# A two-block transformer kernel: the RWKV inverse from 16-wide blocks, and scan work that moves from GpSimd to VectorE

## Chip, cores and metric
One core of one Trainium2 chip runs the whole program in one launch. The metric is the device time of that execution in microseconds; lower is better.

## What is computed
Two blocks of two layers each on a sequence of 256 tokens with 1024 features, in fp32. Block one has a hybrid mixer, cross attention, a dense feed-forward layer and a mixture of eight experts; block two has an attention layer, an MLP, an RWKV-7 layer and a second MLP. The change touches the RWKV layer alone. Its core is a scan that runs forwards (d = 0) and backwards (d = 1) over the tokens, for 16 heads of 64 features:

```
def rwkv7_scan(r, w, k, v, kk, a):
    def step(state, inp):
        r_t, w_t, k_t, v_t, kk_t, a_t = inp
        sa = einsum('bhvk,bhk->bhv', state, -kk_t)
        state = (state * w_t[:, :, None, :] + sa[..., None] * (kk_t * a_t)[:, :, None, :]
                 + v_t[..., None] * k_t[:, :, None, :])
        return state, einsum('bhvk,bhk->bhv', state, r_t)
...
for d in range(2):
    ...
    o = rwkv7_scan(*ins)
    bonus = sum(rh * kd * r_k, axis=-1, keepdims=True) * vh
    dir_out.append((group_norm(o, gn_w, gn_b) + bonus.reshape(nB, S, D)) * g)
y = dir_out[0] + dir_out[1]
return y @ w_o
```

## The kernel before
The scan is done in chunks of 64 tokens: four chunks, two directions. Inside a chunk the recurrence is a triangular system with a 64x64 matrix per head. The stages of `rwkv` follow one another:

- `rwkv_inputs` (L1364): the projections for receptance, keys, values, decay and gates, by matmuls on TensorE with weights that are split into a high and a low part (L335, L336, L372). It ends with the values vx (L1446, L1447) and the gate's inner projection gT (L448, L1449). `rwkv_low` (L1452) makes the decay and the in-context rate of one direction.
- `rwkv_blocks` (L1475), once per direction: eight groups of two heads. For each, ScalarE takes exponentials, VectorE and GpSimd multiply (L1521 to L1529), TensorE makes the chunk matrices (L1540), VectorE masks them (L1548, L1549), and five DMAs on SP's queue write them to a DRAM scratch `rwscr` (L1553 to L1557). The strictly triangular matrices stay in SBUF as nt (L1545, L1546).
- `rwkv_inverse` (L1565), once per direction: it inverts the unit triangular 64x64 matrices of all heads and chunks. Each one is cut into two 32-wide diagonal blocks. VectorE transposes all blocks so that one partition holds one row position (L1579), solves by substitution in 31 steps of a multiply and an add (L1585, L1587), and transposes back in two forms, xn and xd (L1590, L1591). TensorE then forms the off-diagonal 32x32 block in two small products per matrix (L1600, L1608), which run through one partition group at a time, with ScalarE copies between (L1602, L1610). The result xt is a block-diagonal 128x128 matrix for two heads, which is why it is first set to zero (L1578, GpSimd).
- `rwkv_offset` (L1619), once per chunk: everything of the output that doesn't depend on the scan. The gate's outer projection (L1634, TensorE), and the bonus, the norm's shift and the gate's products, almost all on GpSimd (L1625 to L1644). It also takes the mean off the values (L1627 to L1629).
- `rwkv_chunk` (L1648), for each of four steps once per direction: load of the chunk's matrices (mc, L1657), decay of the state (L1666 on VectorE, L1668 on GpSimd), product with the state (pw), product with the inverse (pu, L1685), new state (L1705) and output (po).
- `rwkv_norm` (L1713), once per step and direction: square on ScalarE, mean, a reciprocal root of twelve small VectorE operations (`rsqrt`, L275 to L294), a product on VectorE (L1721) and two operations on GpSimd, in the last step on VectorE (L1723, L1724).

Then the output is transposed (L1357), multiplied with w_o, and the last MLP follows.

The order of instructions on each engine is fixed at build time: a planner takes operations by priority, where priority is place in the program unless `high_priority(n)` moves a part n places ahead, and plays the engines against a timing model. Both calls of the inverse stand ahead by 800 places. Memory sets limits: lxd and lz (L1588, L1592) have one buffer each, in the pool `ip`, for both directions; the second direction's working tile lies in the pool `kp`, over memory that the blocks have used, and in a buffer that the chunk loads use later (L1315). PSUM has two "mm" banks, two "tr" banks and four "acc" banks.

Of the kernel before, what the change touches and what calls it, by code (L numbers as in the profile page):

```python
# [19 lines left out]
P = 128  # L20
D = 1024
KD = 8
# [86 lines left out]
def constants():  # L109
# [104 lines left out]
class K:  # L214
# [1052 lines left out]
    def rwkv(self, h, hstack, hp):  # L1267
# [5 lines left out]
        with ExitStack() as ctx:  # L1273
# [5 lines left out]
            with ExitStack() as left:  # L1279
                with ExitStack() as right:  # L1280
# [11 lines left out]
                    with self.dense("c", 2, 4, "right", 3):  # L1292
                        lp, vx, gT = self.rwkv_inputs(h, rT, z0, z1, tT, aT, opened,
                                                      lambda lp: self.rwkv_low(bq, lp, 0, tT, aT))
# [3 lines left out]
                    xt = [cp.tile([P, KD * 4, P], F32, name="xt0")]  # L1298
# [9 lines left out]
                    with tc.high_priority(800):  # L1308
                        self.rwkv_inverse(ip, ip.tile([P, 3, 32, 32], F32, name="lanes", tag="lanes"), 0, nt[0], xt[0])
                y = lp.tile([P, KD, 4, 64], F32, name="ry")  # L1310
                with ExitStack() as right:
                    kp = pool(right, "rwk", "right")
                    xt.append(kp.tile([P, KD * 4, P], F32, name="xt1"))
# [15 lines left out]
                    for i, c in enumerate((0, 3, 1, 2)):  # L1329
# [4 lines left out]
                        gw[c] = self.rwkv_offset(kp, t[:, i % 2], c, vx, gT, bon, gn, g2, y)  # L1334
# [3 lines left out]
                    for i in range(4):  # L1338
# [4 lines left out]
                        for d, (po, c) in enumerate(outs):  # L1343
                            self.rwkv_norm(kp, po, c, gw[c][d], y, i == 3)
# [19 lines left out]
    def rwkv_inputs(self, h, rT, z0, z1, tT, aT, opened, low):  # L1364
# [5 lines left out]
        with self.tc.tile_pool(name="rin", bufs=1, side="right", reuse_waits="tile") as mp:  # L1370
# [79 lines left out]
        return lp, vx, gT  # L1450
# [114 lines left out]
    def rwkv_inverse(self, lp, lanes, d, nt, xt):  # L1565
# [12 lines left out]
        nc.gpsimd.memset(xt, 0.0)  # L1578
        nc.vector.transpose(n.rearrange("p t s -> p (t s)"), nt[:, :, 32 * a:32 * a + 32].rearrange("p q t -> p t q"))  # L1579
        for s in (range(31) if d == 0 else range(31, 0, -1)):  # L1580
            ts = slice(s + 1, 32) if d == 0 else slice(0, s)
            js = slice(0, s + 1) if d == 0 else slice(s, 32)
            nt_, nj = ts.stop - ts.start, js.stop - js.start
            tv = tmp[:, :nt_ * nj].rearrange("p (t j) -> p t j", t=nt_)
            nc.vector.tensor_mul(tv, n[:, ts, s:s + 1].to_broadcast([P, nt_, nj]),  # L1585
                                 x[:, s:s + 1, js].to_broadcast([P, nt_, nj]))
            nc.vector.tensor_add(x[:, ts, js], x[:, ts, js], tv)  # L1587
# [3 lines left out]
        nc.vector.transpose(xd.rearrange("p q t -> p t q"), x.rearrange("p t j -> p (t j)"))  # L1591
        zs = lp.tile([P, 32, 32], F32, name="lz")  # L1592
        cb = slice(32 * b, 32 * b + 32)
        zb = [self.bank(t) for t in ("mm", "mm", "tr", "tr")]
        for q0 in (0, 16):
            z = zb[q0 // 16]
            for par in range(2):
                pa, pb = pr(par, a), pr(par, b)
                for q in range(16):
                    nc.tensor.matmul(z[pb, q * 32:(q + 1) * 32], nt[pa, q0 + q, cb],  # L1600
                                     xn[pa, q0 + q], start=True, stop=True, skip_group_check=True)
                last = nc.scalar.copy(zs[pb, q0:q0 + 16], z[pb].rearrange("p (q j) -> p q j", q=16))  # L1602
        for q0 in (0, 16):
            z = zb[2 + q0 // 16]
            for par in range(2):
                pa, pb = pr(par, a), pr(par, b)
                for q in range(16):
                    nc.tensor.matmul(z[pa, q * 32:(q + 1) * 32], zs[pb, q0 + q], xd[pb, q0 + q],  # L1608
                                     start=True, stop=True, skip_group_check=True)
                nc.scalar.copy(xt[pa, q0:q0 + 16, 64 * par + 32 * b:64 * par + 32 * b + 32], z[pa].rearrange("p (q j) -> p q j", q=16))  # L1610
        with self.tc.issue_after(last.ins):
            for i in range(4):
                ps = slice(32 * i, 32 * i + 32)
                if d == 0 or i % 2 == 0:
                    nc.scalar.copy(xt[ps, :, ps], xd[ps])
                else:
                    nc.vector.tensor_copy(xt[ps, :, ps], xd[ps])

    def rwkv_offset(self, kp, gate, c, vx, gT, bon, gn, g2, y):  # L1619
# [6 lines left out]
        m = self.sm.tile([P, KD], F32, name="vm")  # L1626
        nc.vector.reduce_sum(m, vx[:, :, c], axis=AX.X)  # L1627
        nc.vector.tensor_scalar(m, m, 1.0 / 64, None, op0=OP.mult)
        nc.gpsimd.tensor_sub(vx[:, :, c], vx[:, :, c], m[:, :, None].to_broadcast([P, KD, 64]))  # L1629
        out = []  # L1630
        for d in range(2):
            b = self.bank("acc", 4)
# [3 lines left out]
            g = gate[:, d]  # L1636
            nc.scalar.copy(g, b.rearrange("p (f v) -> p f v", f=KD))
            nc.gpsimd.tensor_add(vb[d], vb[d], gn[1])
            if d == 0:
                nc.gpsimd.tensor_mul(y[:, :, c], vb[d], g)  # L1640
            else:
                nc.gpsimd.tensor_mul(vb[d], vb[d], g)
                nc.gpsimd.tensor_add(y[:, :, c], y[:, :, c], vb[d])
            nc.gpsimd.tensor_mul(g, g, gn[0])  # L1644
            out.append(g)
        return out

    def rwkv_chunk(self, kp, mp, d, i, prev, scr, xt, pc, vx, hot):  # L1648
# [14 lines left out]
        if prev is not None:  # L1663
# [4 lines left out]
            nc.gpsimd.tensor_mul(st, prev, pcb)  # L1668
# [15 lines left out]
        for f in range(KD):  # L1684
            nc.tensor.matmul(pu[:, f], xt[:, f * 4 + c], w[:, f], start=True, stop=True, skip_group_check=True)  # L1685
# [27 lines left out]
    def rwkv_norm(self, kp, po, c, gw, y, last):  # L1713

        nc = self.nc
        o, sq = (kp.tile([P, KD, 64], F32, name=n, bufs=b) for n, b in (("ro", 2), ("rq", 1)))
        nc.scalar.activation(sq, po, AF.Square)
        va = self.sm.tile([P, KD], F32, name="gva")
        nc.vector.reduce_sum(va, sq, axis=AX.X)
        r = self.rsqrt(va, KD, 1.0 / 64, 64e-5)  # L1720
        nc.vector.tensor_mul(o, po, r[:, :, None].to_broadcast([P, KD, 64]))  # L1721
        eng = nc.vector if last else nc.gpsimd
        eng.tensor_mul(o, o, gw)  # L1723
        eng.tensor_add(y[:, :, c], y[:, :, c], o)  # L1724
# [83 lines left out]
```

## Time and profile before

| | us |
|---|---|
| three runs: lowest, median, highest | 2703.27, 2704.24, 2707.18 |
| the profiled execution's own time | 2704.2 |
| its span in the trace | 2702.4 |

The times are of the device; the trace is of one further execution. An engine's row says how long it was busy; its name stands ahead (PE is TensorE's matmuls, PEld its weight loads, DVE VectorE, ACT ScalarE, POOL GpSimd, SP the engine that issues the DMAs). A granted clock of 1.00 is 2.4 GHz, 0.50 is 1.2 GHz. Time in brackets is idle time ahead of an instruction and what ended it.

### The profile page before, as it was taken

How to read it: one execution, taken by the hardware profiler on the slowest of the kernel's cores; microseconds unless marked ns; L12 is line 12 of the kernel's file. 1: busy time of each engine (PE TensorE's matmuls, PEld its weight loads, DVE VectorE, ACT ScalarE, POOL GpSimd, SP SyncE). 2: the span in 40 equal slices, each digit the busy share in tenths (PEclk: the TensorE clock that was granted, in tenths of full speed). 3: DMA queues.
4: the chain of work that ended last, by engine and by line, in shares of the span. 5: the costliest groups of instructions: out<-in, count | busy, mean ns of one | idle time of the engine just before them, and what ended most of it. 6: DMA issues, size and time to landing. Idle time of an engine off the chain costs nothing. (4 is left out here: it accounts for less than half of the span.)

```text
span 2702.4 us, 38657 instructions
## 1 busy us (share of the span) xinstructions
PE 2470.9 (91%) x14672; PEld 2127.8 (79%) x14672; DVE 2061.6 (76%) x3025; ACT 1557.5 (58%) x2136; POOL 431.1 (16%) x361
## 2 busy tenths in 40 slices
PE   8889999889999999999999999798997788577998
PEld 7778998868788888888888878587996766376897
DVE  8955556955699899988889898666557959967655
ACT  5445445335577778777777777455444646343443
POOL 3800110830000000000000000000111346542111
PEclk9989999989999999999999999899997888668999
DMA  6433454433699999999999999443553227424452
GB/s 239 166 119 131 172 187 161 132 134 133 218 359 368 332 357 368 344 351 351 354 336 360 355 358 353 147 161 107 174 187 106 98 83 191 118 108 190 161 188 104
DMA packets 229952, 598.69 MB, mean 222 GB/s; under 512 B 14778, under 2 KB 33914, under 8 KB 228476
## 3 DMA queue, kind: packets, MB, share of 16 engines
q1 hardware_dynamic: 229756, 596.12, 63.0%
q8 instruction: 117, 1.92, 0.3%
q14 instruction: 79, 0.65, 0.1%
HBM read 579.27 MB, written 16.81 MB: 221 GB/s over the span
## 5 line engine op out<-in xcount | busy, mean ns | idle before, releaser
L336 DVE TENSOR_TENSOR wl<-wst,wh 128x1024 fp32r<-128x1024 f32 (+2 forms) x1037 | 1254.5, 1230 | 351.7 <-ACT wh L335 333.4
L335 ACT ACTIVATE wh<-wst 128x1024 fp32r<-128x1024 f32 (+2 forms) x1037 | 1077.6, 1055 | 562.3 <-PE ps_mm L372 300.3
L372 PE MATMUL ps_mm<-xT_h,wh 128*128 128x256 f32 x1496 | 434.4, 290 | 28.1 <-DVE xT_l L455 15.4
L372 PE MATMUL ps_mm<-xT_h,wl 128*128 128x256 f32 x1496 | 431.6, 289 | 4.7 <-DVE wl L336 3.8
L372 PE MATMUL ps_mm<-xT_l,wh 128*128 128x256 f32 x1496 | 431.8, 289 | 0.2 <-DVE xT_l L455 0.2
L372 PE MATMUL ps_mm<-wh,gh 128*128 128x512 f32 x880 | 352.1, 400 | 0.0
L372 PE MATMUL ps_mm<-wl,gh 128*128 128x512 f32 x880 | 343.8, 391 | 0.0
L372 PE MATMUL ps_mm<-wh,gl 128*128 128x512 f32 x880 | 343.3, 390 | 0.0
L372 PEld LDWEIGHTS ps_mm<-xT_h,wh 128*128 128x128 f32 x1496 | 295.2, 197 | 35.3 <-DVE xT_l L455 16.3
L372 PEld LDWEIGHTS ps_mm<-xT_h,wl 128*128 128x128 f32 x1496 | 294.8, 197 | 8.5 <-DVE wl L336 5.7
L372 PEld LDWEIGHTS ps_mm<-xT_l,wh 128*128 128x128 f32 x1496 | 294.4, 197 | 1.1 <-DVE xT_l L455 0.4
L372 PEld LDWEIGHTS ps_mm<-wl,gh 128*128 128x128 f32 x880 | 165.1, 188 | 35.7
L372 PEld LDWEIGHTS ps_mm<-wh,gl 128*128 128x128 f32 x880 | 165.5, 188 | 32.7
L372 PEld LDWEIGHTS ps_mm<-wh,gh 128*128 128x128 f32 x880 | 165.3, 188 | 32.9 <-ACT gh L363 0.4
L1150 POOL MEMSET qz<- 64x2048 f32 x1 | 1.8, 1799 | 1159.9 <-DVE gg L1158 1159.9
L372 PE MATMUL ps_acc<-wh,mal 128*128 128x512 f32 x448 | 179.1, 400 | 2.8 <-DVE mal L364 2.8
L372 PE MATMUL ps_acc<-wh,mah 128*128 128x512 f32 x448 | 179.0, 400 | 0.7 <-ACT mah L363 0.7
L372 PE MATMUL ps_acc<-wl,mah 128*128 128x512 f32 x448 | 177.7, 397 | 0.0
L372 PE MATMUL ps_acc<-wh,al 128*128 128x512 f32 x344 | 134.8, 392 | 0.0
L372 PE MATMUL ps_acc<-wl,ah 128*128 128x512 f32 x344 | 134.5, 391 | 0.0
L1259 POOL TENSOR_TENSOR mq<-mr 128x512 f32<-128x512 f32 x32 | 56.2, 1758 | 489.5 <-DVE mr L1257 489.5
L372 PE MATMUL ps_acc<-wh,ah 128*128 128x512 f32 x344 | 116.4, 396 | 2.5 <-ACT ah L363 2.5
(469 smaller groups left out, 4061.9 us busy)
## 6 DMA issues: line engine op xcount, KB each, us to landing
wst<-in_moe_gate SPq DMA_DIRECT2D x112, 1024.0 KB, 6.0
wst<-in_moe_down SPq DMA_DIRECT2D x112, 1024.0 KB, 5.6
wst<-in_moe_up SPq DMA_DIRECT2D x112, 1024.0 KB, 5.6
wst<-in_mlp SPq DMA_DIRECT2D x64, 1024.0 KB, 4.9
wst<-in_mix_in SPq DMA_DIRECT2D x16, 1024.0 KB, 5.0
mc<-rwscr SPq DMA_DIRECT2D x8, 1792.0 KB, 7.3
wst<-in_ffn_gate SPq DMA_DIRECT2D x11, 1024.0 KB, 4.9
wst<-in_ffn_up SPq DMA_DIRECT2D x11, 1024.0 KB, 5.1
```

The lines of the kernel that those rows point to most:

```text
L335: nc.scalar.activation(wh[:, :n], src, AF.Copy)
L336: nc.vector.tensor_sub(wl[:, :n], src, wh[:, :n])
L372: self.nc.tensor.matmul(out, a, b, start=start and i == 0, stop=stop and i == n - 1, skip_group_check=True)
L1150: nc.gpsimd.memset(qz[64:128, :, 0], 0.0)
L1259: nc.gpsimd.tensor_mul(q, r, r)
```

## The change
The 32-wide diagonal blocks are no longer solved whole. VectorE solves two 16-wide blocks inside each in 15 steps, both in one instruction. TensorE then merges twice: the two 16-wide blocks into a 32-wide one, in the two forms that are needed (z1, z3 and z2, new), and the two 32-wide ones into the 64-wide inverse (as before). All these loops now run over the matrices and inside that over two or four partition groups, so that consecutive matmuls are of different groups. They take their PSUM from the two "mm" banks. xt holds only the 64x64 matrices, without the zeros, so that the product with it in `rwkv_chunk` becomes two 64-wide ones. The first direction's inverse has no raised priority any more, the second's is raised by 1600 places.

The gates' products go to ScalarE (bonus) and VectorE, reading the projection from PSUM; the means of the values are taken once, at the end of `rwkv_inputs`; the decay product goes to VectorE; the norm takes both directions of a step together, with one reciprocal root for both, and stays on VectorE.

```diff
+        c.add(f"half{d}", (i % 32 // 16 != d).astype(np.float32))
...
-                    with tc.high_priority(800):
-                        self.rwkv_inverse(ip, ip.tile([P, 3, 32, 32], F32, name="lanes", tag="lanes"), 0, nt[0], xt[0])
+                    self.rwkv_inverse(ip, ip.tile([P, 3, 32, 32], F32, name="lanes", tag="lanes"), 0, nt[0], xt[0])
...
-                    with tc.high_priority(800):
+                    with tc.high_priority(1600):
...
+            vm = lp.tile([P, KD, 4], F32, name="vm")
+            nc.vector.reduce_sum(vm, vx, axis=AX.X)
+            nc.vector.tensor_scalar(vm, vm, 1.0 / 64, None, op0=OP.mult)
+            nc.vector.tensor_sub(vx, vx, vm[:, :, :, None].to_broadcast([P, KD, 4, 64]))
...
-        nc.gpsimd.memset(xt, 0.0)
+        for par in range(2):
+            nc.gpsimd.memset(xt[pr(par, b), :, 32 * a:32 * a + 32], 0.0)
...
-        for s in (range(31) if d == 0 else range(31, 0, -1)):
...
+        for s in (range(15) if d == 0 else range(15, 0, -1)):
...
+            tv = tmp[:, :2 * nt_ * nj].rearrange("p (u t j) -> p u t j", u=2, t=nt_)
+            xv = two(x, t0, [32, nt_], j0, [1, nj])
+            nc.vector.tensor_mul(tv, two(n, t0, [32, nt_], s, [0, nj]), two(x, s, [0, nt_], j0, [1, nj]))
+            nc.vector.tensor_add(xv, xv, tv)
...
+        for q in range(32):
+            for ps in grp:
+                nc.tensor.matmul(z1[ps, q], nt[ps, q, 32 * a:32 * a + 32], xn[ps, q, low], start=True, stop=True,
+                                 skip_group_check=True)
+        nc.scalar.activation(zh[:, :, low], z1, AF.Copy, scale=self.c(f"half{d}"))
+        z3 = self.bank().rearrange("p (q j) -> p q j", q=32)
+        for q in range(32):
+            for par in range(2):
+                ps = pr(par, a)
+                nc.tensor.matmul(z3[ps, q], xd[ps, q], zh[ps, q, low], start=True, stop=True, skip_group_check=True)
...
+            nc.vector.tensor_add(xn[ps, :, low], xn[ps, :, low], z3[ps])
+        z2 = self.bank().rearrange("p (q j) -> p q j", q=32)
+        for q in range(32):
+            for ps in grp:
+                nc.tensor.matmul(z2[ps, q], zh[ps, q], xd[ps, q, high], start=True, stop=True, skip_group_check=True)
+        nc.vector.tensor_add(xd[:, :, high], xd[:, :, high], z2)
...
-        vb = [kp.tile([P, KD, 64], F32, name="vb", tag="ro", bufs=2) for _ in range(2)]
-        for d in range(2):
-            nc.gpsimd.tensor_mul(vb[d], vx[:, :, c], bon[d][:, :, c:c + 1].to_broadcast([P, KD, 64]))
...
+            nc.vector.tensor_mul(mb, vm[:, :, c], bon[d][:, :, c])
+            vb = kp.tile([P, KD, 64], F32, name="vb", tag="ro", bufs=2)
+            for f in range(KD):
+                nc.scalar.activation(vb[:, f], vx[:, f, c], AF.Identity, scale=bon[d][:, f, c:c + 1],
+                                     bias=mb[:, f:f + 1])
...
+            nc.vector.tensor_mul(gate[:, d], b, gn[0])
+            nc.vector.tensor_add(vb, vb, gn[1])
             if d == 0:
-                nc.gpsimd.tensor_mul(y[:, :, c], vb[d], g)
+                nc.vector.tensor_mul(y[:, :, c], vb, b)
             else:
...
+                nc.vector.tensor_mul(vb, vb, b)
+                nc.vector.tensor_add(y[:, :, c], y[:, :, c], vb)
...
-            nc.gpsimd.tensor_mul(st, prev, pcb)
+            nc.vector.tensor_mul(st, prev, pcb)
...
-            nc.tensor.matmul(pu[:, f], xt[:, f * 4 + c], w[:, f], start=True, stop=True, skip_group_check=True)
+            for par, own, other in sides:
+                nc.tensor.matmul(pu[own, f], xt[own, f * 4 + c], w[own, f], start=True, stop=True,
+                                 skip_group_check=True)
...
+        r = self.rsqrt(va, 2 * KD, 1.0 / 64, 64e-5)
+        for d, (po, c) in enumerate(outs):
+            o = kp.tile([P, KD, 64], F32, name="ro", bufs=2)
+            nc.vector.tensor_mul(o, po, r[:, d * KD:(d + 1) * KD, None].to_broadcast([P, KD, 64]))
+            nc.vector.tensor_mul(o, o, gw[c][d])
+            nc.vector.tensor_add(y[:, :, c], y[:, :, c], o)
```

## Rows read from the trace of the kernel before

**Rows 1.** The page, its head.

```profile
span 2702.4 us, 38657 instructions
```

**Rows 2.** Stretches: length, busy us of PE, PEld, DVE, ACT, POOL; granted clock, DMA.

```profile
2211.00:2259.00 48.00, 39.12 (x233) 31.99 (x232) 38.21 (x74) 35.44 (x102) 37.45 (x59) 0.89 0.61 132
2261.50:2321.50 60.00, 39.01 (x230) 34.06 (x228) 58.10 (x116) 31.68 (x92) 31.96 (x40) 0.83 0.70 182
2321.50:2326.00 4.50, 0.00 (x0) 0.00 (x0) 0.00 (x0) 0.00 (x0) 0.00 (x0) 0.50 0.92 190
2326.00:2412.00 86.00, 53.46 (x738) 43.86 (x740) 70.32 (x108) 28.98 (x47) 57.40 (x46) 0.58 0.24 82
2412.00:2468.30 56.30, 43.68 (x841) 40.07 (x841) 44.67 (x117) 19.22 (x33) 21.01 (x15) 0.86 0.34 128
```

**Rows 3.** Chain of waits from 2317 to 2475 us, shares by line.

```profile
by line: DVE lanes L1587 18.4%; DVE lanes L1585 16.8%; DVE rs L1666 9.0%; PE ps_mm L1600 4.4%; PE ps_tr L1608 4.2%; issue 3.3%; DVE rs_y L294 3.3%; PE ps_tr L1357 3.1%; DVE gva L1719 2.8%; DVE rs_q L293 2.6%; DVE lanes L1590 2.5%; PE ps_acc
```

**Rows 4.** Timeline of VectorE: start us, duration us, line, operation, out<-in.

```profile
2261.73 0.19 DVE L1585 TENSOR_TENSOR lanes<-lanes 128x31 f32<-128x31 f32 x1
...
2326.01 1.93 DVE L1579 STREAM_TRANSPOSE lanes<-nt 128x1024 f32<-128x1024 f32 x1 [4.57 <-DMA rwscr<-mt]
...
2332.96 1.27 DVE L1587 TENSOR_TENSOR lanes<-lanes 128x156 f32<-128x156 f32 x1
...
2357.32 0.32 DVE L1585 TENSOR_TENSOR lanes<-lanes 128x156 f32<-128x156 f32 x1
```

**Rows 5.** Timeline of GpSimd.

```profile
2332.77 1.28 POOL L1638 TENSOR_TENSOR vb<-vb,gn 128x512 f32<-128x512 f32 x1
...
2367.03 1.27 POOL L1640 TENSOR_TENSOR ry<-vb,gwb 128x512 f32<-128x512 f32 x1 [9.91 <-ACT gwb L1637]
```

**Rows 6.** Stretches, writes to the tile lanes alone: PE, PEld, DVE, POOL; clock, DMA.

```profile
2261.50:2321.50 60.00, 0.00 (x0) 0.00 (x0) 21.06 (x42) 0.00 (x0) 0.83 0.70 182
2326.00:2390.50 64.50, 6.00 (x128) 5.76 (x128) 58.17 (x86) 1.10 (x2) 0.61 0.23 80
```

**Rows 7.** Groups of instructions from 2100 to 2500: busy us, mean ns, idle before.

```profile
L1521 POOL TENSOR_TENSOR zt<-z,e 128x256 f32<-128x256 f32 x32 | 26.3, 832 | 9.9 <-DVE bk L1522 7.2 <-ACT pc L1514 1.9 <-ACT mt L1551 0.5
L1520 ACT ACTIVATE aw<-ra,zg,zf 128x256 f32<-128x256 f32 x32 | 18.4, 596 | 16.3 <-DVE bk L1522 15.8
L1666 DVE TENSOR_TENSOR rs<-sn,pc 64x512 f32<-64x512 f32 x12 | 14.3, 1194 | 0.3
...
L1514 ACT ACTIVATE pc<-ps_mm 128x4 f32<-128x4 f32 x16 | 2.9, 182 | 0.0
```

**Rows 8.** Timeline of SP's queue, first and last of 18 DMA issues.

```profile
2306.09 0.57 SPq L1555 DMA_DIRECT2D rwscr<-mt  x1
...
2321.76 0.61 SPq L1557 DMA_DIRECT2D rwscr<-mt  x1
```

**Rows 9.** Timeline of TensorE: merges of the inverse, and a product of the scan.

```profile
2368.85 3.62 PE L1608 MATMUL ps_tr<-lxd,lz 32*32 32x32 f32 x64
...
2398.17 0.26 PE L1608 MATMUL ps_tr<-lxd,lz 32*32 32x32 f32 x1
...
2398.35 0.24 PE L1608 MATMUL ps_tr<-lxd,lz 32*32 32x32 f32 x1
...
2411.86 1.97 PE L1689 MATMUL ps_acc<-st,mc 64*64 64x64 f32 x32
```

**Rows 10.** Timeline of ScalarE: the last piece of xt.

```profile
2411.35 0.58 ACT L1610 COPY xt<-ps_tr 32x512 f32<-32x512 f32 x1 [1.13 <-PE ps_tr L1608]
```

**Rows 11.** Timeline of VectorE: a reciprocal root's first and last step, the last norm operation.

```profile
2463.70 0.17 DVE L279 TENSOR_SCALAR rs_v<-gva 128x8 f32<-128x8 f32 x1
...
2465.71 0.17 DVE L294 SCALAR_TENSOR_TENSOR rs_y<-rs_q,rs_y 128x8 f32<-128x8 f32 x1
...
2467.46 0.69 DVE L1724 TENSOR_TENSOR ry<-ry,ro 128x512 f32<-128x512 f32 x1
```

**Rows 12.** Timeline of VectorE at the end of the inputs.

```profile
2211.09 0.85 DVE L273 TENSOR_SCALAR gT<-gT 128x512 f32<-128x512 f32 x1 [10.49 <-ACT gT L272]
```

More of the change, by code (lines that the diff above doesn't have):

```diff
@@ L1591, in rwkv_inverse @@
         nc.vector.transpose(xd.rearrange("p q t -> p t q"), x.rearrange("p t j -> p (t j)"))
+        low, high = (slice(0, 16), slice(16, 32)) if d == 0 else (slice(16, 32), slice(0, 16))
+        zh = lanes[:, 0]
+        nc.vector.memset(zh[:, :, high], 0.0)
+        z1 = self.bank().rearrange("p (q j) -> p q j", q=32)
+        grp = [slice(32 * g, 32 * g + 32) for g in range(4)]
+        for q in range(32):
+            for ps in grp:
+                nc.tensor.matmul(z1[ps, q], nt[ps, q, 32 * a:32 * a + 32], xn[ps, q, low], start=True, stop=True,
+                                 skip_group_check=True)
@@ new lines, in rwkv_inverse @@
+        nc.scalar.activation(zh[:, :, low], z1, AF.Copy, scale=self.c(f"half{d}"))
[4 more added lines that the diff above has]
+                nc.tensor.matmul(z3[ps, q], xd[ps, q], zh[ps, q, low], start=True, stop=True, skip_group_check=True)
+        for par in range(2):
+            ps = pr(par, a)
+            nc.vector.tensor_add(xn[ps, :, low], xn[ps, :, low], z3[ps])
+        z2 = self.bank().rearrange("p (q j) -> p q j", q=32)
@@ L1592, in rwkv_inverse @@
+        for q in range(32):
+            for ps in grp:
+                nc.tensor.matmul(z2[ps, q], zh[ps, q], xd[ps, q, high], start=True, stop=True, skip_group_check=True)
+        nc.vector.tensor_add(xd[:, :, high], xd[:, :, high], z2)
         zs = lp.tile([P, 32, 32], F32, name="lz")
         cb = slice(32 * b, 32 * b + 32)
-        zb = [self.bank(t) for t in ("mm", "mm", "tr", "tr")]
+        sides = [(pr(par, a), pr(par, b)) for par in range(2)]
         for q0 in (0, 16):
[L1596 to L1602, printed above, removed]
@@ L1603, in rwkv_inverse @@
-        for q0 in (0, 16):
[L1604 to L1619, printed above, removed]
-        nc = self.nc
-        vb = [kp.tile([P, KD, 64], F32, name="vb", tag="ro", bufs=2) for _ in range(2)]
-        for d in range(2):
-            nc.gpsimd.tensor_mul(vb[d], vx[:, :, c], bon[d][:, :, c:c + 1].to_broadcast([P, KD, 64]))
[L1626 to L1629, printed above, removed]
+            z = self.bank().rearrange("p (q j) -> p q j", q=16)
@@ new lines, in rwkv_inverse @@
+            for q in range(16):
+                for pa, pb in sides:
+                    nc.tensor.matmul(z[pb, q], nt[pa, q0 + q, cb], xn[pa, q0 + q], start=True, stop=True,
+                                     skip_group_check=True)
+            for pa, pb in sides:
+                nc.scalar.copy(zs[pb, q0:q0 + 16], z[pb])
+        for pa, pb in sides:
+            nc.scalar.copy(xt[pa, :, 32 * a:32 * a + 32], xd[pa])
+            nc.vector.tensor_copy(xt[pb, :, 32 * b:32 * b + 32], xd[pb])
@@ new lines, in rwkv_inverse, with rwkv_offset @@
+        for q0 in (0, 16):
+            z = self.bank().rearrange("p (q j) -> p q j", q=16)
+            for q in range(16):
+                for pa, pb in sides:
+                    nc.tensor.matmul(z[pa, q], zs[pb, q0 + q], xd[pb, q0 + q], start=True, stop=True,
+                                     skip_group_check=True)
+            for pa, pb in sides:
+                nc.scalar.copy(xt[pa, q0:q0 + 16, cb], z[pa])
+    def rwkv_offset(self, kp, gate, c, vx, vm, gT, bon, gn, g2, y):
+        nc = self.nc
@@ L1711, in rwkv_chunk, with rwkv_norm @@
         return nxt, po, c
-    def rwkv_norm(self, kp, po, c, gw, y, last):
+    def rwkv_norm(self, kp, outs, gw, y):
         nc = self.nc
[L1716 to L1724, printed above, removed]
+        va = self.sm.tile([P, 2 * KD], F32, name="gva")
+        for d, (po, c) in enumerate(outs):
+            sq = kp.tile([P, KD, 64], F32, name="rq")
+            nc.scalar.activation(sq, po, AF.Square)
+            nc.vector.reduce_sum(va[:, d * KD:(d + 1) * KD], sq, axis=AX.X)
+        r = self.rsqrt(va, 2 * KD, 1.0 / 64, 64e-5)
+        for d, (po, c) in enumerate(outs):
+            o = kp.tile([P, KD, 64], F32, name="ro", bufs=2)
+            nc.vector.tensor_mul(o, po, r[:, d * KD:(d + 1) * KD, None].to_broadcast([P, KD, 64]))
+            nc.vector.tensor_mul(o, o, gw[c][d])
+            nc.vector.tensor_add(y[:, :, c], y[:, :, c], o)
 def body(tc, d, cat, fat, stage=None):
```

36 lines of the change are left out of this document (15 added, 21 removed).

## The prediction

> **What bounds the kernel now.** I read the page first: one core, a span of 2702.4 us [rows 1]. Then I cut the span into stretches around the code that the diff touches, and read engine times there [rows 2]. The blocks of the second direction run until about 2321.5 us, with VectorE busy 58.1 of 60.0 us. Then comes a hole of 4.5 us in which no engine works. The next 86 us, to 2412, hold the rest of the first inverse, the whole second one, the gates and one and a half chunks of the scan: VectorE is busy 70.3, TensorE 53.5 (granted clock 0.58 on average, so mostly at the lower of its two levels, 1.2 GHz), ScalarE 29.0 and GpSimd 57.4 us. The rest of the scan takes 56.3 us, VectorE busy 44.7.
>
> The third view is the chain of waits over this stretch [rows 3]: the two VectorE lines of the inverse (L1585, L1587) make 35% of it, more than anything else. So time here is VectorE's: either its own work, or a short TensorE or ScalarE step between two pieces of it.
>
> The fourth is VectorE's timeline [rows 4]. The second inverse starts at 2326.01, released by the last block's write to DRAM. One and the same form, 128x156, takes 1.27 us at 2332.96 and 0.32 us at 2357.32. GpSimd explains it [rows 5]: at 2332.77 it is in a 1.28 us TENSOR_TENSOR of the gates, and before 2367.03 it had sat idle for 9.9 us. An inverse step that meets a GpSimd instruction of the gates lasts about as long as that instruction does. Added up [rows 6]: writes to the inverse's buffer cost VectorE 21.1 us among the blocks (42 steps) and 58.2 us after 2326 (82 steps and 4 transposes).
>
> **The change part by part.** Times are against the profiled execution, 2704.2 us, 1.8 us above its own span; the median of the three runs is 2704.24, so the two agree. "End" is the end of the scan, 2468.3.
>
> *Shorter solve.* 62 VectorE steps a direction become 30, with at most 128 elements each: 15 multiplies and 15 adds. Step t works on two blocks of t(16-t) elements, 91 on average. [Rows 4] has 0.19 us for 31 elements and 0.32 for 156; between them, with some 0.04 from one end to the next start, I take 0.29 a step, 8.7 us a direction, when GpSimd is quiet.
>
> *Among the blocks.* The first inverse loses its priority but its input is there before the second direction's blocks. 30 steps at the mean of the 42 (0.50 us) are 15 us where 21.1 stood. Bounds for what the stage gains: 12 us at best, as the first direction's blocks take 48.0 us where these take 60.0 [rows 2]; minus 4 at worst, if each of the 30 meets a GpSimd product of the blocks (0.83 [rows 7]). The first inverse's matmuls now also use only the two "mm" PSUM buffers, which the blocks use too; I give that no price of its own. SP speaks for a small gain: its last 18 writes, from 2306.09 to 2321.76, are issued back to back [rows 8], and the second inverse's buffer still waits for the last of them. I take 3: that inverse starts at 2323 instead of 2326. Its higher priority cannot bring it forward, since its memory is only free then.
>
> *Second inverse, solve.* A transpose of 1.93 [rows 4], 8.7 of steps and two more transposes: 14.5 us, to 2337.5. The GpSimd memset of xt shrinks and no gate work stands in its queue.
>
> *Merges.* Per direction 128 calls in z1, 64 in z3, 128 in z2 and 64 in each of the two old stages: 448 calls. Each fp32 call stands in the trace as two instructions: 64 calls a direction before, 256 instructions for both. So 896 instead of 128. [Rows 9] has 64 in one partition group in 3.62 us, 57 ns each; and a run of seven that alternate between two groups, from 2398.17 to 2398.35, 30 ns each. The new loops alternate two or four groups, half of them with 16 columns instead of 32. I bound an instruction at 15 ns (the alternating price halved again for four groups) and 57, and take 25, near the alternating row. 896 x 25 = 22.4 us, plus ScalarE's copies that stand in the chain (about five of 0.58 [rows 10], with handoffs 4.6): 27 us, to 2364.5.
>
> In these loops all groups write one PSUM bank; in the alternating row the two stages write two banks. The nearest row with one bank is L1689, 64x64 from alternating halves, 32 in 1.97 us, 62 ns [rows 9]: twice the columns of the 32-wide instruction for almost its price, so halves do overlap there. The Trainium skill (TensorEngine Tiling (Array Packing), Restrictions and Gotchas) says that different row tiles cannot access one PSUM bank at the same time. By it nothing would overlap, and the merges would cost 55 us a direction; L1689 is against it. It is the slower rival below.
>
> *Shared buffers.* lxd and lz have one buffer each for both inverses. Whichever writes lxd first holds it until its merges end. If the first inverse gets through during the blocks and the hole, the second waits 0 to 10 us; if not, the first comes 27 us behind. I take 5: the last piece of xt lands at 2369.5 where it lands at 2411.9 now [rows 10]. Behind a transpose that waits for lxd, VectorE's queue holds the gates and then the scan's products; those wait too.
>
> *Gates.* They leave GpSimd: per chunk seven VectorE operations on 128x512 at 0.69 [rows 11] plus two tiny ones of 0.17, 20.7 us for four chunks, and 64 ScalarE activations of 128x64. Their price lies between 0.18 (128x4) and 0.60 (128x256) [rows 7]; by columns 0.28, so 18 us. ScalarE has 57 of 86 us free there [rows 2], so it is hidden; at 0.60 it would be 38 and some 8 us would come out. VectorE's part lies beside the merges, which leave VectorE about 25 us. Cover gone, it costs up to 20.7.
>
> *Moved means.* The mean of v and its subtraction go to before the blocks, at most 5.6 us of VectorE (eight times the 0.69 of [rows 11]). VectorE waits 10.5 us there before 2211.09 [rows 12], so I cost it at nothing; without cover it costs 5.6. Nothing is added to a DMA queue.
>
> *Scan.* VectorE takes over five decay products and ten norm operations, the 15 that GpSimd does after 2412 [rows 2]: 15 x 0.69 = 10.4. It loses three of seven reciprocal roots, 2.2 us each by the first and last step of one [rows 11], 6.6; the slowing of ten products L1666, at 1.19 where 0.69 is what such an operation takes alone [rows 11], 5 (L1666 in [rows 7]); and the same slowing of some small operations, about 3. So minus 4: 52.3 instead of 56.3, bounds minus 12 and plus 8 (gates spilling over).
>
> *Sum.* 2369.5 + 52.3 = 2421.8, so 46 us less by the chain. A check by load: from 2323 VectorE has 17 (second inverse), 8 (rest of the first), 20.7 (gates), 16.5 (scan) and 4 x 7.7 (norms), 93 us: 2416 with no idle time. Now it is idle for 27 of 142 us [rows 2]. With 16 idle it ends at 2432. I take 2430: 38 us less, **2666 us**.
>
> **The rivals.**
> - *Merges in a row.* The second inverse takes lxd, the first merges behind it: last piece at 2337.5 + 27 + 2 + 27 = 2393.5, end near 2446, less 22 us: 2682. For it: one buffer, and the priority given to the second. Against: the first's input is ready 60 us earlier.
> - *VectorE keeps its idle time.* The gates don't fit beside the merges: 2323 + 93 + 27 = 2443, less 25: 2679. For it: now also a fifth of VectorE's time is waiting, although GpSimd carries the gates.
> - *No overlap in one bank.* 896 x 57 ns = 51 us and 4 of copies, both directions in a row: 2337.5 + 55 + 2 + 55 = 2449.5, end 2501.8, 34 us **slower**: 2738. It decides from about 38 ns an instruction, where the last piece lands at 2415.9, four later than now because the scan is four shorter: (2415.9 - 2337.5 - 2 - 9) / 1792. For it: the 57 ns row. Against: L1689.
> - *No difference.* The merges at about 38 ns, or several gains given back to the blocks: 2700 to 2709.
>
> **How the numbers follow.** A measurement here can tell about 0.2%, 5.4 us, from no change. Forecast 0.60 (2652 to 2678), merges in a row 0.20, idle time kept 0.08, no difference 0.05, no overlap 0.07. Faster 0.88, same 0.05, slower 0.07. The range, 2650 to 2690, reaches from the load check with no idle time (end 2414 to 2416) over the first three cases.
>
> **What would show it.** Right: VectorE steps of the inverse at 0.2 to 0.3 us after 2326 with GpSimd almost silent; the last piece of xt near 2370; a z1 of 256 instructions in 5 to 8 us; VectorE over 85% busy from the blocks' end to the scan's. Wrong: z1 near 14 us; the two merges one behind the other; blocks that end after 2326; scan chunks of more than 14 us.

## The result, and the profile after

Four runs of the changed kernel have a median of 2676.94 us (2675.02 to 2679.11), four of the kernel before 2703.76 (2702.81 to 2707.18): ratio 0.990, 95% interval 0.9888 to 0.9913, so 26.8 us faster. The forecast was 2666 with a range of 2650 to 2690: right in sign and range, 11 us too low.

The profiled execution took 2676.23, its span is 28.1 us shorter. Nearly all of that is there at the end of the scan: 2438.7 where it was 2468.2. The page's head and its queue of instructions, and beneath them the stretches that answer to [rows 2]: length, busy us of PE, PEld, DVE, ACT, POOL, granted clock, DMA share, GB/s. The third ends with the last piece of xt.

```profile
span 2674.3 us, 41421 instructions
...
PE 2466.7 (92%) x16080; PEld 2119.1 (79%) x16080; DVE 2026.9 (76%) x2972; ACT 1574.4 (59%) x2192; POOL 353.5 (13%) x305
...
q8 instruction: 128, 2.10, 0.3%
```

```profile
2261.50:2321.50 60.00, 45.42 (x664) 39.58 (x664) 52.23 (x106) 35.84 (x104) 32.08 (x40) 0.84 0.72 183
2321.50:2326.00 4.50, 2.66 (x194) 2.55 (x187) 1.28 (x3) 4.43 (x10) 0.23 (x1) 0.50 0.89 214
2326.00:2380.50 54.50, 36.94 (x1277) 27.29 (x1271) 36.61 (x75) 32.45 (x73) 2.71 (x4) 0.63 0.27 93
2380.50:2438.70 58.20, 43.79 (x1112) 38.81 (x1108) 43.66 (x104) 23.99 (x42) 0.00 (x0) 0.88 0.43 157
```

The blocks end where they did, though VectorE is 5.9 us less busy in them. The second inverse, from its start to the last piece of xt, takes 54.8 us where it took 85.9: 31 us come from there. From that piece to the scan's end it is 58.2 us where it was 56.3: two are given back. GpSimd is all but silent after 2326, and VectorE, forecast at over 85% busy up to the scan's end, is busy for 67% and 75% of the last two stretches. It no longer sets the pace. The chain of waits from 2317 to 2445, which answers to [rows 3], has "issue" in the first place where the two lines of the solve stood:

```profile
by line: issue 11.6%; PE ps_acc L1661 7.1%; PE ps_mm L1642 5.8%; DVE rs L1692 5.4%; DMA gn<-in_rk_gn 5.3%; PE ps_tr L1356 4.8%; PE ps_mm L1699 3.3%; PE ps_mm L1705 2.9%; PE ps_mm L1631 2.8%; PE ps_mm L1622 2.8%; ACT rs L1720 2.7%; PE ps_acc
```

What this issue time is can be seen in TensorE's timeline of the second inverse's merges (start us, duration us, line, out<-in, count, and in brackets the idle time ahead with what ended it):

```profile
2345.13 1.25 PE L1608 MATMUL ps_mm<-lanes,nt 32*32 32x16 f32 x121
2347.98 1.21 PE L1608 MATMUL ps_mm<-lanes,nt 32*32 32x16 f32 x124 [1.60 <-issue]
...
2351.45 1.49 PE L1642 MATMUL ps_mm<-lxd,lz 32*32 32x32 f32 x48 [2.20 <-issue]
2352.88 4.42 PE L1661 MATMUL ps_acc<-g,gT 128*64 128x512 f32 x12
...
2357.83 2.11 PE L1615 MATMUL ps_mm<-lanes,lxd 32*32 32x16 f32 x122
...
2364.94 1.90 PE L1622 MATMUL ps_mm<-lxd,lanes 32*32 32x16 f32 x128 [4.49 <-issue]
2368.41 1.15 PE L1622 MATMUL ps_mm<-lxd,lanes 32*32 32x16 f32 x72 [1.57 <-issue]
...
2372.04 2.19 PE L1631 MATMUL ps_mm<-lanes,nt 32*32 32x32 f32 x75 [1.17 <-issue]
```

The four-group matmuls of z1 come every 10 ns (121 in 1.25 us), those of z2 every 15, those of z3 (two groups) every 17, the two old stages' every 30. But after 128 of them, a lot in what follows, TensorE stands still, mostly for 1.2 to 5.4 us, with "issue" as the reason: it waits for nothing that the profile shows. The next lot begins 3.47 us behind the last (2364.94 to 2368.41, and 2347.98 to 2351.45), whether its work takes 1.9 us or 1.3. From 2324 to 2383 there are nine such gaps, 19.7 us; the longest, 5.40 us, starts at 2326.2 inside the first inverse's z2. The kernel before has none from 2326 to 2412 and 0.7 us in the scan.

**My theory** for the experiments: these are waits for instructions. The page's instruction queue q8 moved 128 packets of 16.4 KB (before: 117). Matmuls and weight loads together are 2 x 16080, which is 125.6 lots of 256; before, 2 x 14672 or 114.6. So a packet seems to hold 256 of TensorE's instructions, 128 matmuls with their weight loads, just the length of a burst. (What the trace's records of these packets show stands at the end of the section on the prediction.) The rivals: the shared buffers, and ScalarE's order. In its timeline zh (L1610) starts at 2355.05, well behind z1's end at 2349.2, because 24 activations of the gates stand ahead of it:

```profile
2346.97 8.06 ACT L1657 ACTIVATE vb<-vx,vmb,bon 128x64 f32<-128x64 f32 x24 [2.24 <-DVE ry L1670]
2355.05 0.69 ACT L1610 ACTIVATE lanes<-ps_mm,cons 128x512 f32<-128x512 f32 x1
```

### The profile page after: what moved, and what is told of

Same layout as the page of the kernel before. It is cut to its first block, busy times and chain, and to the rows that moved or that the text cites. A ratio compares the mean times of both kernels' runs of the same rounds, so it can differ in the third digit from the quotient of the medians.

```text
span 2674.3 us, 41421 instructions
## 1 busy us (share of the span) xinstructions
PE 2466.7 (92%) x16080; PEld 2119.1 (79%) x16080; DVE 2026.9 (76%) x2972; ACT 1574.4 (59%) x2192; POOL 353.5 (13%) x305
```

## The experiments

### One half of the change at a time

new_inverse_old_gates keeps the new inverse and puts the gates, decay, norm and means back:

```diff
-            nc.vector.tensor_mul(st, prev, pcb)
+            nc.gpsimd.tensor_mul(st, prev, pcb)
...
-                        self.rwkv_norm(kp, outs, gw, y)
+                        for d, (po, c) in enumerate(outs):
+                            self.rwkv_norm(kp, po, c, gw[c][d], y, i == 3)
```

> The changed kernel with the gates, the decay product, the norms and the means as they were in the kernel before (GpSimd); only the new inverse stays. If the steps of the inverse are again held up by GpSimd: 30 steps of the second direction at about 0.70 us instead of 0.29 (12 us) and the scan 4 us longer, so about 2693 us. Rival, the inverse alone brings the gain (its shorter chain finds GpSimd's gaps): 2677 to 2682 us.

Measured 2690.62 us, ratio 0.9947 (0.9931 to 0.9964). The first reading holds, GpSimd holds VectorE up. VectorE's work on the tile lanes in the second inverse is 26.0 us in 36 instructions; in the changed kernel it is 14.9 in as many:

```profile
2326.00:2400.00 74.00, 18.51 (x1021) 17.48 (x1013) 26.03 (x36) 0.69 (x1) 1.11 (x2) 0.65 0.24 78
```

```profile
2326.00:2384.00 58.00, 16.13 (x935) 15.09 (x927) 14.90 (x36) 0.69 (x1) 0.89 (x2) 0.62 0.26 88
```

The second fence is the changed kernel. The slowing by GpSimd costs VectorE 11.1 us here (12 expected). From the second inverse's start to the last piece of xt it is 62.7 us instead of 54.8, 7.8 more, and the scan is 4.6 us longer (4 expected).

old_inverse_new_gates has the old inverse, its priorities and the wide xt, with the new gates:

```diff
-        for s in (range(15) if d == 0 else range(15, 0, -1)):
+        for s in (range(31) if d == 0 else range(31, 0, -1)):
...
-                    with tc.high_priority(1600):
+                    with tc.high_priority(800):
```

> The kernel before's inverse with its priorities, and the changed kernel's gates, decay, norms and means (VectorE and ScalarE). If GpSimd was what made the steps long, the 82 steps and 4 transposes after the blocks fall from 58.2 us to about 82 x 0.32 + 8 = 34 us, and the gates' 20.7 us on VectorE come on top: about 2690 to 2700 us. Rival, the gates alone bring most of the gain: below 2685 us, with a merge of about 57 ns a matmul that TensorE's instruction supply can follow.

Measured 2684.27 us, ratio 0.9923 (0.9907 to 0.994), 6 us under the expected range and just inside the rival's. The solve came as worked out, 35.1 us in 87 instructions (expected 34; 58.2 in [rows 6]). What I had not counted is the overlap behind it: two of the forward direction's products with its xt (L1688) stand ahead of the second inverse's last merge (L1613), and there is no issue gap:

```profile
2368.19 3.68 PE L1688 MATMUL ps_acc<-rw,xt 128*128 128x64 f32 x16 [1.96 <-ACT rw L1684]
...
2379.71 2.00 PE L1688 MATMUL ps_acc<-rw,xt 128*128 128x64 f32 x16 [0.69 <-ACT rw L1684]
...
2398.77 2.23 PE L1613 MATMUL ps_tr<-lxd,lz 32*32 32x32 f32 x64
```

From the last piece of xt (2401.6) to the scan's end it is 47.4 us here, 58.2 in the changed kernel. The halves bring 14.3 and 20.7 us by the medians, 35 if they added up; together they bring 26.8. The scan shows where much of it goes: from the second inverse's start to the last piece of xt the changed kernel is 17.3 us faster than this one (54.8 against 72.1), and its scan is 10.8 us slower.

### What alternating is worth

```diff
-        for q in range(32):
-            for ps in grp:
+        for ps in grp:
+            for q in range(32):
                 nc.tensor.matmul(z1[ps, q], nt[ps, q, 32 * a:32 * a + 32], xn[ps, q, low], ...
```

and so in all five loops (groups_in_turn).

> The changed kernel with the loops of every merge turned: all 32 (16) blocks of one partition group, then the next group; same calls, same count. If alternation is what makes them short, a matmul goes from 10 to 16 ns back to about 57 ns: 896 x 57 = 51 us a direction instead of about 27 with the gaps, so the second direction's merges end some 20 us later, about 2697 us, and the gaps in which TensorE waits for nothing shown are gone, because 128 matmuls then last 7 us, longer than its instructions take to come. Rival, the supply of instructions sets the pace in either order: 2677 to 2682 us, gaps as before.

Measured 2700.99 us, ratio 0.9992 (0.9982 to 1.0001): without the alternation nothing of the gain is left. z1's matmuls take 40 ns, z2's 52, where the changed kernel has 10 and 15 (z2 at a granted clock of 0.50 in both, z1 at 0.71 here and 1.00 there). TensorE is busy for all of the 79.3 us up to the last piece of xt, and there is no issue gap:

```profile
2326.00:2405.30 79.30, 79.30 (x1465) 69.58 (x1465) 37.09 (x76) 33.51 (x75) 1.21 (x3) 0.56 0.18 60
```

```profile
2354.12 10.10 PE L1608 MATMUL ps_mm<-lanes,nt 32*32 32x16 f32 x250
...
2377.46 12.93 PE L1622 MATMUL ps_mm<-lxd,lanes 32*32 32x16 f32 x250
```

The matmuls and the 128 packets are the same, but a lot of 128 now lasts 5 to 7 us, longer than the 3.5 in which one came before.

### Buffers and order

own_buffers:

```diff
-        xd = lp.tile([P, 32, 32], F32, name="lxd", tag="lxd", bufs=1)
+        xd = lp.tile([P, 32, 32], F32, name="lxd", tag="lxd" if d == 0 else "lxe", bufs=1)
...
-        zs = lp.tile([P, 32, 32], F32, name="lz")
+        zs = lp.tile([P, 32, 32], F32, name="lz", tag="lz" if d == 0 else "ly")
```

> The changed kernel with a buffer of its own for each direction's lxd and lz. If the shared buffer is what costs, the second inverse's second transpose comes at about 2343 us instead of 2353.7 and the end of the scan 8 to 10 us earlier: about 2668 us. Rival, TensorE's instructions come at 3.5 us or more for each 128 matmuls, and both directions' merges queue for that: the transpose comes earlier, the end at most 4 us earlier, 2673 to 2677 us, and the gaps stay.

Measured 2678.14 us, ratio 0.9901 (0.9884 to 0.9919). The second transpose follows the first at once, 7.5 us earlier, and nothing comes of it:

```profile
2344.45 1.93 DVE L1598 STREAM_TRANSPOSE lanes<-lanes 128x1024 f32<-128x1024 f32 x1
2346.23 1.92 DVE L1599 STREAM_TRANSPOSE lxd<-lanes 128x1024 f32<-128x1024 f32 x1
```

zh_first puts vb behind zh on ScalarE, zh_first_own_buffers does both:

```diff
-        nc.scalar.activation(zh[:, :, low], z1, AF.Copy, scale=self.c(f"half{d}"))
+        self.zh = nc.scalar.activation(zh[:, :, low], z1, AF.Copy, scale=self.c(f"half{d}"))
...
+                with self.tc.issue_after(self.zh.ins) if c in (1, 2) else nullcontext():
```

> The changed kernel with one order added on ScalarE: the 32 activations vb of the chunks 1 and 2 come behind the second inverse's eviction zh. In the changed kernel zh starts at 2355.05, 5.8 us after z1's last matmul, behind 24 vb activations. With lxd still shared, its second transpose ends at 2355.7 all the same, so z3 can start 2 us earlier at most: 2674 to 2677 us. Rival, zh's place was all of the delay: 5 us less, 2672 us.

> Both: zh ahead of vb, and a buffer of its own for each direction's lxd and lz. If order and buffer each hide the other, z3 starts at about 2352 instead of 2357.8 and the end is 6 us earlier: 2671 us. Rival, the supply of TensorE's instructions: the same 128-matmul packets have to come, z3 and z2 then run into longer gaps, and no more than 3 us is gained: 2674 us or more.

Measured 2675.97 (ratio 0.9894, 0.9877 to 0.991) and 2677.01 us (0.9899, 0.9882 to 0.9915). Neither wait was worth anything on its own, nor both together. With both, z3 starts at 2353.87 instead of 2357.83, but z2 then runs into a gap of 5.30 us, and the last piece of xt comes at 2381.0 (2380.5 in the changed kernel).

### Fewer instructions, less data beside them

half_the_instructions: z3, z2 and the last stage read bf16 copies, so that these three merges have bf16 inputs; a call is then one matmul instruction.

```diff
+        xr = lp.tile([P, 32, 32], BF16, name="lxr", tag="lxr", bufs=1)
+        nc.scalar.copy(xr, xd)
+        zh = lp.tile([P, 32, 32], BF16, name="lzh", tag="lzh", bufs=1)
...
-        zs = lp.tile([P, 32, 32], F32, name="lz")
+        zs = lp.tile([P, 32, 32], BF16, name="lz")
```

> z3, z2 and the last merge stage (256 of the 448 calls of a direction) read bf16 copies, so that a call is one matmul instruction instead of two: 256 fewer a direction, two lots of 128; one ScalarE copy (1.1 us) and one VectorE addition (0.7 us) a direction come in, and the products of these stages are of bf16 precision. If TensorE waits for its instructions, two lots less are 7 to 12 us of a direction, and the second direction's stand on the path: 2667 to 2672 us, with gaps still after each 128 matmul instructions. Rival, the gaps are tied to something else (a bank, the matmuls themselves): at most 256 x 15 ns = 3.8 us less and 1.8 us more: 2675 us.

Measured 2671.38 us, ratio 0.9876 (0.986 to 0.9893), 5.6 less by the medians, at the edge of what was expected. 512 matmuls fewer, and q8 has 124 packets instead of 128, one for 128 matmuls. From 2318 to 2385 the issue gaps fall from 19.8 us to 6.0. In this trace ScalarE's order holds zh back until 2359.79, 6.6 us behind z1's end; what that costs is tried below.

small_g2_load takes away the transfer that was issued at 2322.70, just ahead of the longest gap:

```diff
-                    nc.sync.dma_start(g2, self.d["rk_g2"].rearrange("d p c -> p d c"))
+                    nc.gpsimd.memset(g2, 0.0)
+                    nc.sync.dma_start(g2[:, :, 0:32], self.d["rk_g2"].rearrange("d p c -> p d c")[:, :, 0:32])
```

> Only 32 of the 1024 columns of g2 are loaded, GpSimd fills the others with zeros, so the gates are left out for the rest: the 1 MB transfer that is issued at 2322.7, just ahead of the longest gap (5.40 us from 2326.2), is gone. If instructions queue behind data on the DMA engines, that gap shrinks to the 1.2 to 2.2 us of the gaps without data beside them, and the end comes up to 3 us earlier. Rival, the gap is not a matter of traffic: it stays at 4 to 6 us.

A single run took 2674.09 us, 0.9 below the lowest of the changed kernel's four, so the time decides nothing. The gap tells more. It is 2.39 us here, 5.40 in the changed kernel, and 4.86 (no_hot) to 6.23 us (own_buffers) in the five other kernels that have this stage in fp32 with alternating groups and load all of g2. The gap in the second z2, which no edit touched, keeps its length:

```profile
2328.72 0.41 PE L1623 MATMUL ps_mm<-lxd,lanes 32*32 32x16 f32 x17 [2.39 <-issue]
...
2364.24 1.90 PE L1623 MATMUL ps_mm<-lxd,lanes 32*32 32x16 f32 x128 [4.50 <-issue]
```

That one begins at 2360.45 in the changed kernel, beside a load of mc that SP's queue issued there at 2357.34 (1792 KB, 8.4 us to landing). Gaps with no load beside them are at most 2.5 us.

### Towards a faster kernel

half_zh_first joins half_the_instructions with zh_first; half_zh_first_own also gives the second inverse buffers of its own:

```diff
-                        self.rwkv_inverse(ip, t[:, 0:3072]...
+                        self.rwkv_inverse(kp, t[:, 0:3072]...
```

> The bf16 stages and zh ahead of vb on ScalarE, lxd and lz still shared. With half the instructions in three stages, z1 was over at 2353.2 and zh started at 2359.79, behind 24 vb activations (8.06 us). If TensorE's instructions were what hid this order in the fp32 kernels (where zh first brought 1 us), it now counts: z3 starts 5 to 6 us earlier, about 2665 us. Rival, the same chain is held by another thing as before (the gates' matmuls, banks): 2669 to 2672 us.

> As the one before, and the second direction's inverse has buffers of its own. In the kernel with half the instructions lxd's second transpose already followed the first at once (2347.86 behind 2346.05), so the shared buffer no longer costs: the same time as with shared buffers, within 3 us. Rival, the buffer is a second hidden wait: 4 us less than with shared buffers, about 2661 us.

Measured 2670.74 (ratio 0.9879, 0.9863 to 0.9896) and **2664.35 us** (0.9853, 0.9836 to 0.9869). The main reading missed in both: the first time lies in its rival's range, the second below the range and above its rival's figure. zh now starts right behind z1, and z2's addition (L1625) starts 3.6 us behind z2's end (2358.5), behind gate products that wait for vb. In half_zh_first_own:

```profile
2360.21 0.69 DVE L1671 TENSOR_TENSOR ry<-vb,ps_acc 128x512 f32<-128x512 f32 x1
2360.81 0.69 DVE L1669 TENSOR_TENSOR vb<-vb,gn 128x512 f32<-128x512 f32 x1
2361.53 0.69 DVE L1673 TENSOR_TENSOR vb<-vb,ps_acc 128x512 f32<-128x512 f32 x1
2362.14 0.68 DVE L1625 TENSOR_TENSOR lxr<-lxd,ps_mm 128x512 bf16<-128x512 f32 x1
```

That looks like the next wait, but TensorE's next stage (L1634) needs z3's addition and not z2's. After three matmuls it stands in an issue gap beside a load of mc, until 0.8 us after z2's addition is done (2362.82):

```profile
2360.32 0.28 PE L1634 MATMUL ps_mm<-lanes,nt 32*32 32x32 f32 x3 [1.79 <-DVE lanes L1620]
2363.66 1.86 PE L1634 MATMUL ps_mm<-lanes,nt 32*32 32x32 f32 x61 [3.05 <-issue]
```

Where the 6.4 us between the two medians come from stays open. The profile of half_zh_first is of its fastest execution (2666.90 us, the other three took 2670.30 to 2672.12), that of half_zh_first_own of its slowest (2665.25), so the profiles are only 1.65 us apart. In them the way from the inverse's start to the last piece of xt is 48.8 and 47.8 us, so the buffers do little there. The scan behind it takes 62.1 and 55.9, and in its first 11 us the granted clock is 0.69 and 0.92, but the inverse also starts 5.7 us earlier in the first.

no_hot leaves out the eight matmuls that nobody reads:

```diff
-                            ... hot if (i, d) == (0, 1) else None)
+                            ... None)
```

> The changed kernel without the eight 128x512 matmuls that stand in chunk 0 of the second direction and whose result nobody reads. They take 3.78 us (2382.77 to 2386.55) between pw and pu. If they only stand in the way, the scan starts 3 us earlier: about 2674 us. Rival, they keep the granted clock up (mean 0.62 before 2384, 0.90 after): without them the scan's matmuls run at the lower clock, 62 ns instead of 34 in pairs, and each chunk step takes some 3 us longer: 2683 us or more.

Measured 2672.34 us, ratio 0.9886 (0.987 to 0.9903): 4.6 less by the medians, though the ranges just touch (2671.12 to 2675.60 against 2675.02 to 2679.11). From the last piece of xt to the scan's end it is 53.3 us instead of 58.2, at a mean granted clock of 0.92 (0.88 with them). In this kernel they only stand in the way.

gates_behind is half_zh_first_own without the eight, and with the gates of two chunks behind the inverse on both queues:

```diff
+                        with ExitStack() as late:
+                            if i >= 2:
+                                late.enter_context(tc.issue_after(self.xa.ins))
+                                late.enter_context(tc.issue_after(self.zh.ins))
```

(xa is z2's addition.)

> The kernel with bf16 stages and own buffers, without the eight unread matmuls, and with the gates of chunks 1 and 2 behind the second inverse on both queues: their ScalarE operations behind zh, their VectorE operations behind z2's addition. In the run before this one the wait had moved from zh to that addition: z2 ended at 2358.5 and the addition started at 2362.14, behind VectorE's gate products that wait for vb. The unread matmuls were worth 4.6 us by themselves, so 2664.4 - 4.6 = 2660 us without a gain from the order. If the order counts, the addition follows z2 within 0.5 us, the end comes 3 us earlier still, and the gates fill the 18 us in which VectorE waits at the scan's start: about 2657 us. Rival, these gates then stand in the scan's own VectorE queue, at 14 operations of 0.69 us: 2660 to 2668 us.

Measured 2672.09 us, ratio 0.988 (0.9864 to 0.9897): missed, 8 us worse than half_zh_first_own. The addition does follow z2 by 0.4 us (2357.22), but TensorE then has an issue gap of 4.43 us, beside an mc load. From z1's end to the end of that gap it is 9.1 us with either order, and the last piece of xt comes 48.4 us behind the inverse's start (47.8). The vb activations now stand among the scan's own copies on ScalarE, and the forward product waits 3.1 us for rw. The scan takes 60.6 us. In its first 11 us the granted clock is 0.69 where half_zh_first_own had 0.92. The order of the gates and the missing eight matmuls are not told apart here, and the 4.6 us of no_hot do not carry over to this kernel.

## Why the prediction was right, and where it was off

- **What bounds the kernel; GpSimd slows VectorE's steps.** Right: old_inverse_new_gates' solve takes 35.1 us where it took 58.2, new_inverse_old_gates' steps lose 11.1. Solve steps are 0.19 to 0.29 us with GpSimd silent, forecast 0.29. Wrong in what was to follow: VectorE doesn't stay the engine that sets the pace (67% and 75% busy, forecast over 85%).
- **Among the blocks.** Forecast: the inverse starts at 2323. It starts at 2325.66. VectorE does have 5.9 us less work there, but SP's writes run to 2320.74 (2321.76 in [rows 8]); the 3 us were not there to take.
- **Solve, done at 2337.5.** z1 starts at 2345.04, 7.5 us later. 2.7 of them are the later start. The steps were priced well, but not what stands between them on VectorE's queue: four operations of the gates (2.7 us) and three of the first inverse's merges (2.1 us); GpSimd's fills hold the first step up by 1.2 us. One of the two back-transposes that were counted ahead of z1 came behind its start.

```profile
2325.66 1.94 DVE L1584 STREAM_TRANSPOSE lanes<-nt 128x1024 f32<-128x1024 f32 x1 [3.21 <-issue]
2328.85 0.20 DVE L1594 TENSOR_TENSOR lanes<-lanes 128x30 f32<-128x30 f32 x1 [1.20 <-POOL lanes L1579]
2331.77 1.29 DVE L1665 TENSOR_TENSOR vb<-vb,gn 128x512 f32<-128x512 f32 x2 [0.21 <-DMA gn<-in_rk_gn]
2335.17 1.39 DVE L1637 COPY xt<-lxd 32x1024 f32<-32x1024 f32 x2
2342.40 1.95 DVE L1598 STREAM_TRANSPOSE lanes<-lanes 128x1024 f32<-128x1024 f32 x1
```

- **Merges, 896 x 25 ns = 22.4, 27 with copies.** This step failed, in its form more than in its number. From z1's start (2345.04) to the last copy (2380.5) it is 35.5 us, against 32 with the 5 for the shared buffer. The matmuls themselves are cheaper than the price taken, 10 to 30 ns, and z1 lies below the lower bound of 15. What they cost is a lot of 128 every 3.47 us at best, 27 ns each, and more beside a transfer. Seven lots of 128 are 24 us; the loads of mc add about 3 in the 4.49 us gap, and the gates' 12 and the scan's matmuls stand in between. No bound of mine was a supply; that 25 ns lies near the 27 that it allows is luck. The 896 are right, but they stand against 256 a direction in the kernel before, not 128 (L1600 and L1608 run 256 instructions each for both).
- **No overlap in one bank**, the slower rival at 2738. It fell. By the Trainium skill (TensorEngine Tiling (Array Packing), Restrictions and Gotchas) z1's four groups in one bank should take turns; the trace disagrees: z2, which also has four groups in one bank, takes 15 ns a matmul with groups alternating and 52 with groups in turn, both at a granted clock of 0.50 (z1 10 and 40 ns, but at 1.00 and 0.71). But its break-even of 38 ns was about right: at 40 to 52 ns groups_in_turn gains nothing.
- **Shared buffers, 5 us.** The wait was longer, 9.4 us (2344.35 to 2353.74), and worth nothing: own_buffers takes it away without gain. It lasts until the first inverse's last merge (L1642, 2351.45 to 2352.94). So z3 and z2 of the second do stand behind the merges of the first, which the prediction named as a sign of being wrong, and the time lies between its 2666 and the 2682 of *Merges in a row*. But own_buffers shows that the shared buffer, from which that rival draws the row, is not what costs.
- **Gates hidden.** VectorE's part is, but for the 2.7 us among the solve's steps. ScalarE's 64 activations took 21.8 us (forecast 18) and were hidden by load, but not by place: they stand ahead of zh. Yet moving them behind zh gains only 1.0 us by the medians in zh_first, within the spread, and 0.6 in half_zh_first.
- **Moved means.** Right: nothing; gT's wait is 10.49 us as in [rows 12].
- **Scan, 52.3.** It takes 58.2, or 14.6 us for each of the four chunks; more than 14 was named as a sign of being wrong. The products L1692 came down from 1.19 to 0.69 us as forecast and VectorE has 1.0 us less to do (44.67 to 43.66) instead of 4 less. What I left out is the head start. In the kernel before, the forward direction had a chunk and a half behind it when the last piece of xt came: its first product with xt, of sixteen matmuls, began 39 us ahead of that piece, and the product at 2411.86 in [rows 9] is already of its second chunk. In the changed kernel it begins 6 us behind it, as the forward inverse and its chunk now queue among the merges of the second. First the kernel before, then the changed one:

```profile
2372.40 3.67 PE L1685 MATMUL ps_acc<-rw,xt 128*128 128x64 f32 x16
```

```profile
2382.77 3.78 PE L1705 MATMUL ps_mm<-hot 128*128 128x512 f32 x8
2386.48 1.32 PE L1712 MATMUL ps_acc<-rw,xt 64*64 64x64 f32 x32
```

I had seen that chunk and a half in [rows 2] and counted it in the scan of before, but not in that of after. no_hot puts 4.6 us on the eight matmuls that stand ahead of the product; what the lost head start costs by itself was not tried. old_inverse_new_gates, which has the same gates and norms, the eight matmuls and two forward products ahead of its last merge, needs 47.4 us for its scan.

The errors had one sign: 11 us later at the last piece of xt (7.5 ahead of z1, 3.5 behind it), 6 us longer in the scan. The load check, taken for its 16 us of idle time, had pulled the forecast 8 us up from the chain's sum, and so it came out only 11 us off. It counted the load of an engine that no longer sets the pace, so that is luck.

The runs above make it likely that the issue gaps are waits for instructions, and the trace's own records show it. They hold the start and length of each packet of q8, which the views don't list. Five of the nine gaps of the changed kernel, in us:

| TensorE stands still | q8's packet, start to landing | from landing to the next matmul |
|---|---|---|
| 2326.17 to 2331.57 | 2328.93 to 2330.21 | 1.36 |
| 2346.38 to 2347.98 | 2345.54 to 2346.56 | 1.42 |
| 2349.25 to 2351.45 | 2349.03 to 2349.91 | 1.54 |
| 2360.45 to 2364.94 | 2362.63 to 2363.59 | 1.35 |
| 2366.84 to 2368.41 | 2366.08 to 2367.00 | 1.41 |

All nine end 1.2 to 1.6 us behind the landing of a packet, although they last from 0.29 to 5.40 us. And the number of TensorE's instructions in the trace ahead of each (matmuls, weight loads and semaphore waits) differs from gap to gap by 256, 512 or 768: all nine stand at the border of a block of 256. Behind seven of them the next packet starts 1.05 to 1.28 us after the new lot's first matmul. Behind the other two, where data is being moved, it is 4.24 and 4.66 us. From 2332 to 2357 the DMA engines are 0.01 busy; from 2359 to 2363, ahead of the end of the 4.49 us gap, 0.94, and there it is the packet's start that comes late, not its 0.96 us of transfer. So without data beside it a lot takes 1.1 us to the next packet's start, 0.9 for the packet and 1.4 from its landing to the first matmul, however short its own work is: the 3.47 us.

The count of packets agrees (117, 124 and 128 for 14672, 15568 and 16080 matmuls). The Trainium skill (Runtime: NRT & Kernel Launch, Instruction fetch mechanics) gives the same size: 16 KiB blocks of 256 instructions. It calls the cost of crossing a block mostly hidden. The trace disagrees for such short matmuls: 3.47 us a lot against 1.3 to 1.9 us of work.

## What to carry to other kernels

Price a loop of small matmuls twice, by what one costs on the array and by how many instructions it is; here 128 matmuls with their weight loads came no faster than every 3.5 us, and slower beside a big load. For matmuls shorter than 27 ns fewer instructions helped (5.6 us), while buffers of their own and another order on ScalarE brought the changed kernel nothing.

When a wait is taken away and the time stays, look at what the next one is: the shared buffer and ScalarE's and VectorE's orders all show as waits in the traces, and TensorE stood in its issue gaps with or without them.

And matmuls whose result nobody reads should be left out for a trial when the work around them moves.

## What was not expected of the hardware

- TensorE stood still at the border of each 256 instructions, 128 matmuls with their weight loads, when these took less than about 3.5 us: gaps of up to 2.5 us without a load beside them, of up to 6.2 with one. Each of the changed kernel's nine ended 1.2 to 1.6 us behind the landing of a 16 KB packet of the instruction queue.
- Four partition groups that write one PSUM bank, alternating matmul by matmul, gave 15 ns for a 32x32 matmul with 16 columns, group after group 52 ns, both at a granted clock of 0.50.
- Eight 128x512 matmuls ahead of the scan (3.78 us) did not raise its clock: 0.88 with them, 0.92 without.
